# GpSimd's written order ends at the sixth feed-forward pair, and the last spatial-row weights move to activation tiles

## The chip, the cores and the metric

The kernel runs on one core of one Trainium2 chip. The core has five engines with queues of their own: PE (TensorE: matrix products, with its weight loads shown as PEld), DVE (VectorE), ACT (ScalarE), POOL (GpSimd) and SP (SyncE, which only issues transfers). Sixteen DMA engines move data between memory and the on-chip memory. The metric is the time of one execution in microseconds of device time; lower is better.

## The reference

One layer of a diffusion backbone runs over 1024 latent tokens and 256 context tokens of width 1024, all in f32:

```
u    = RMSNorm(x) * (1 + scale1) + shift1
p    = u @ w_in
A    = pooled windows of p (2/4/8/16), minus p, a map per group
B    = su * (W_s RMSNorm(sv) + b)        over chunks of 128 tokens
C    = bidirectional mLSTM, 4 heads of 128, per-head RMSNorm, output gate
x   += gate1 * (sum_r sigmoid(gate_r) * (y_r @ w_branch[r])) @ w_out
x   += gate2 * relu((RMSNorm(x)*(1+scale2)+shift2) @ w_ff1)^2 @ w_ff2
y    = RMSNorm(x)
```

It also returns the final mLSTM states of the context tokens. Branch B's input `sv` (512 columns) is what the code calls the spatial rows. `w_ff1` is 1024 x 4096 and `w_ff2` 4096 x 1024.

## The kernel before

**Arithmetic.** Every large product is made of three matmuls on values split in two: `hi` is the operand cast to the type fp32r by ACT, `lo` is the rest, by a subtraction on DVE; the products are hi·hi, hi·lo and lo·hi. So each weight tile costs one ACT cast and one DVE subtraction before PE can use it.

**Planner.** The kernel is written in a language whose planner simulates the engines' timelines and orders the instructions by what is ready in that simulation, earlier code first. Each engine then executes its own list strictly in order. Two things constrain the planner here: `Pinned` (line 35) wraps an engine so that the instructions issued through it keep their written order on that engine; and buffers come from pools with a fixed number of slots, so that an instruction that writes a new tile waits until a slot of the pool is free.

**Pools that matter.** `sp` has 59 slots of 128x512 f32, the activation tiles (`slot`). `wp` holds raw weights (2 slots), and hi and lo weights of 128x1024 (3 slots each); `load_w` fills them. PSUM has three banks for long products (`ps_mm`) and five for the others (`ps_sd`).

**mLSTM heads and spatial rows.** Four heads run one after the other (`head`), each a chain of short steps over PE, DVE, ACT and GpSimd. While one head runs, the planner fills PE with independent products: the projections of later heads, then the spatial rows, then the projections of the pooling branch (`xp`). The spatial rows are computed in two halves of 256 columns (`q`, line 711); each half has two weight sets (`hf`), for the first and the last four of eight k tiles. For each of ten token tiles 24 matmuls accumulate in a `ps_mm` bank, and ACT copies the result to the row tile `vn` (line 725). In the first half each of the ten groups needs a new `vn` slot. The 40 slots of the modulated input `uT` and three slots `rhl` live through all of this; a head has eight slots of queries, keys and values.

**The first feed-forward matrix.** 16 pairs of 128-column blocks (`fp`, line 1324) go through a Strassen-like scheme with seven products in place of eight (`Pair`, `FeedPair`). After a pair's products, `sums` (line 1274) stores the results and forms their sums on DVE: three stores to `scr_h` and one to `scr_c` from ACT, one to `scr_c` and four to `scr_s` from GpSimd. The sums use tiles of `tmp2`, a pool of six slots, five of which one pair takes. `second_sums(fp)` prepares the weight side of the second matrix: SP loads two rows of `w_ff2` into the z slots 10, 11, 14 and 15 (line 1298), GpSimd makes four subtractions, and GpSimd stores the result to `scr_t`. All pairs share these four z slots, so that the load of one waits for the store of the one before. The dictionary `LATE` (line 1323) says after which pair which `second_sums` are issued: none after pairs 0 and 1, (0) after 2, (1, 2) after 3, (3) after 4, (4, 5) after 5, and from there each after its own pair. The whole loop runs with GpSimd pinned.

**The second feed-forward matrix.** Seven products (`PRODUCTS`, line 1356) run over 16 k steps each; a step needs a right tile (`r_fp`, weights) and a left tile (`l_fp`), each loaded by SP, cast by ACT and split by DVE; every four steps a context tile (`c_j`) joins. In the first product the raw tiles of steps 0 to 9 are loaded into z slots that the first matrix leaves: `FREE` names slots 0, 2, 10, 14, 16, 12, 4, 6, 18, 8 for `r`, the next slot for `l`. So `r_2`, `l_2`, `r_3`, `l_3` use the four slots of `second_sums`. The residual rows are brought back into z by GpSimd's transfers (line 1496).

Of the kernel before, what the change touches and what calls it, by code (L numbers as in the profile page):

```python
# [7 lines left out]
F32 = mybir.dt.float32  # L8
F32R = mybir.dt.float32r
AF = mybir.ActivationFunctionType  # L10
ALU = mybir.AluOpType
# [3 lines left out]
P = 128  # L15
D = 1024
KT = D // P
# [31 lines left out]
def hybrid_step(  # L49
# [6 lines left out]
    nc = tc.nc  # L56
    engines = nc.vector, nc.scalar, nc.gpsimd, nc.tensor
    V, A, G, PE = engines
    SP = nc.sync
# [9 lines left out]
    def slot(name, dt=F32R):  # L69
        return sp.tile([P, 512], dt, tag="s", name=name)  # L70
# [4 lines left out]
    def ps_mm(name):  # L75
        return pp.tile([P, 512], F32, tag="mm", name=name, bufs=3)
# [7 lines left out]
    def fetch_w(src, name):  # L84
        raw = wp.tile([P, 1024], F32, tag="raw", name=f"raw_{name}")
        SP.dma_start(raw, src)
        return raw

    def load_w(src, name, raw=None, eng=V):
        raw = fetch_w(src, name) if raw is None else raw  # L90
        hi = wp.tile([P, 1024], F32R, tag="hi", name=f"hi_{name}", bufs=NHL)
        lo = wp.tile([P, 1024], F32R, tag="lo", name=f"lo_{name}", bufs=NHL)
        A.copy(hi, raw)
        eng.tensor_tensor(lo, raw, hi.bitcast(F32), ALU.subtract)
        return hi, lo
# [10 lines left out]
    def split_part(name, g):  # L106
        if g < 2:
            return slot(f"{name}h{g}"), slot(f"{name}l{g}")
        c = slot(f"{name}c")
        return c[:, 0:256], c[:, 256:512]  # L110
# [16 lines left out]
    def rstd_of(ssq, n, name):  # L127
        r = small([P, 16], f"rs_{name}")
        V.tensor_scalar(r[:, :n], ssq, 1.0 / n_of[name[0]], EPS, ALU.mult, ALU.add)  # L129
        G.tensor_tensor(r[:, :n], r[:, :n], neghalf[:, :n], ALU.pow)  # L130
        return r
# [3 lines left out]
    wt = slot("wt")  # L135
    G.memset(wt.bitcast(F32), 0.0)

# [110 lines left out]
    def busy(n):  # L248

        for _ in range(n):  # L250
            PE.matmul(wps, wt[:, 0:P], wt, start=True, stop=True)
# [23 lines left out]

    V, A, G, PE = (Pinned(tc, e) for e in engines)
    busy(30)
# [87 lines left out]
    def gates_of(g):  # L365


        t0, n = GROUPS[g]
        pg = ps_sd(f"pg{g}")
        for k in range(KT):  # L370
            ahi, alo = uT[k][g]
            w = wgs[k // 4][:, k % 4]
            PE.matmul(pg[:, :n], w, ahi, start=k == 0, stop=False)
            PE.matmul(pg[:, :n], w, alo, start=False, stop=k == KT - 1)
        both, low = slot(f"pgs{g}", F32), slot(f"pgl{g}", F32)
        A.copy(both[:, :n], pg[:, :n])
        SP.dma_start(low[0:100, :n], both[4:104, :n])
        gparts[g] = both, low

    def gates_add(g):  # L380
        t0, n = GROUPS[g]
        both, low = (t[:, :n] for t in gparts[g])
        V.scalar_tensor_tensor(zr[0][:, t0 : t0 + n], both[0:36], bgt[:, 0:1], low[0:36], ALU.add, ALU.add)
        V.tensor_tensor(zr[1][:, t0 : t0 + n], both[64:100], low[64:100], ALU.add)
# [46 lines left out]
    gates_of(2)  # L431
    V, A, G, PE = engines
    gates_add(2)

    def chunks(ap):
        return ap.rearrange("p (c t) -> p c t", t=P)
# [11 lines left out]
    V.scalar_tensor_tensor(zf, zf, 0.0, z4, ALU.min, ALU.subtract)  # L448
    G.memset(z4, 1.0)
    G.memset(chunks(z4)[0:32, :, 0:1], 0.0)  # L450
# [61 lines left out]
    for nm, idx, groups in (("k", I_K, 3), ("v", I_V, 3), ("q", I_Q, 1)):  # L512
        w1, lst = begun[f"{nm}1"] = load_w(w_in[idx + 1], f"{nm}1"), []
        if nm == "q":
            PE = Pinned(tc, nc.tensor)
# [16 lines left out]
    PE = nc.tensor  # L532
# [16 lines left out]
    for g in range(3):  # L549
        t0, n = GROUPS[g]  # L550
        r = slot(f"rhl{g}")
# [154 lines left out]
            qkv = head_proj(h + 1)  # L706


    vn = []
    vsq = cp.tile([P, NT, 2], F32, name="vsq")  # L710
    for q in range(2):
        wq = [load_w(w_sv[q, hf], f"sv{q}_{hf}") for hf in range(2)]
        for i in range(NT):
            g, o = (i * P) // 512, (i * P) % 512
            if q == 0:
                vn.append(slot(f"vn{i}", F32))
            ps = ps_mm(f"sv{q}_{i}")
            for k in range(KT):
                whi, wlo = wq[k // 4]
                s = slice((k % 4) * 256, (k % 4 + 1) * 256)  # L720
                uh, ul = uT[k][g]
                PE.matmul(ps[:, :256], uh[:, o : o + P], whi[:, s], start=k == 0, stop=False)
                PE.matmul(ps[:, :256], ul[:, o : o + P], whi[:, s], start=False, stop=False)
                PE.matmul(ps[:, :256], uh[:, o : o + P], wlo[:, s], start=False, stop=k == KT - 1)
            A.copy(vn[i][:, q * 256 : (q + 1) * 256], ps[:, :256])
            A.activation(ps[:, 256:512], ps[:, :256], AF.Square, accum_out=vsq[:, i, q : q + 1])
    vs1 = small([P, 16], "vs1")[:, :NT]
    V.reduce_sum(vs1, vsq, axis=mybir.AxisListType.X)
    r = rstd_of(vs1, NT, "v")
# [181 lines left out]
    def tmp2(name, dt=F32):  # L911
        return q1.tile([P, 512], dt, tag="s", name=name, bufs=6)
# [158 lines left out]
    for ri, r in enumerate(ORDER):  # L1071
        scr = (scr_ya, scr_yb, scr_yc)[r]
        ys = [[] for _ in range(4)]
        for g in range(3):
            for kc in range(4):
                t0, n = GROUPS[g]
                raw = tmp2(f"yr{r}_{kc}_{g}")
# [5 lines left out]
                hi, lo = split_part(f"y{r}_{kc}", g)  # L1083
# [3 lines left out]
        for d in range(KT):  # L1087
            if d % 2 == 0:
                wb = [load_half(w_branch[r, d // 2][:, i * 512 : i * 512 + 512], f"wb{r}_{d}_{i}") for i in range(2)]
            for g in range(3):  # L1090
# [4 lines left out]
                for kc in range(4):  # L1095
                    yh, yl = ys[kc][g]
                    whi, wlo = wb[kc // 2]
                    o = kc % 2 * 256 + (d % 2) * P
                    s = slice(o, o + P)
# [194 lines left out]
    def second_sums(fp):  # L1294

        q = [zs(i) for i in (10, 11, 14, 15)]
        for r in range(2):
            SP.dma_start(zs(10 + 4 * r, 2), w_ff2[2 * fp + r])
        b11, b12, b21, b22 = q
        for out, x, y in ((b11, b12, b11), (b12, b22, b12), (b22, b22, b11), (b21, b22, b21)):  # L1300
            G.tensor_tensor(out, x, y, ALU.subtract)
        for r in range(2):
            G.dma_start(scr_t[fp][:, 2 * r : 2 * r + 2, :], zs(10 + 4 * r, 2).rearrange("p (q c) -> p q c", c=512))
# [18 lines left out]
    G = Pinned(tc, nc.gpsimd)  # L1322
    LATE = {0: (), 1: (), 2: (0,), 3: (1, 2), 4: (3,), 5: (4, 5)}
    for fp in range(NFP):
# [6 lines left out]
        del pairs[fp]  # L1331
        for late in LATE.get(fp, (fp,)):
            second_sums(late)
    G = nc.gpsimd


    pa.close()
# [262 lines left out]
```

## Time and profile before

| | us |
|---|---|
| median of 3 runs | 1958.27 (1958.17 to 1959.2) |
| the profiled execution | 1958.53 |
| its span in the trace | 1956.7 |
| PE busy | 1906.7 |
| DVE busy | 1309.8 |
| ACT busy | 851.3 |
| POOL busy | 366.6 |

The profile shows one execution. A row of a timeline gives start, length, engine, line, operation, output and input, and in brackets how long the engine was idle before it and what ended that wait. Lines that go through `Pinned` all carry line 43, so operations there are told apart by their tiles. A wait in the trace is put down to what came last.

### The profile page before, as it was taken

To read this page: it belongs to the slowest core of one execution; us is meant where nothing else is said; L and a number is where in the kernel's file an instruction comes from. 1 tells how busy PE (TensorE), PEld (TensorE's weight loads), DVE (VectorE), ACT (ScalarE), POOL (GpSimd) and SP (SyncE) were. 2 spreads that over 40 slices of the span, in tenths; PEclk is the share of its full clock that TensorE was granted. 3 is DMA by queue.
4 is the path that set the end of the run, shared out by engine and by line. 5 is a ranking of instruction groups with operands and counts; after the bars stand their busy time and mean duration, and the time that the engine had idled before them with its cause. 6 is when DMAs were issued, how large, how long until landed. Compare 5 with 4: busy or idle time off the path is not lost.

```text
span 1956.7 us, 28251 instructions
## 1 busy us (share of the span) xinstructions
PE 1906.7 (97%) x10142; PEld 1629.2 (83%) x10142; DVE 1309.8 (67%) x2238; ACT 851.3 (44%) x1771; POOL 366.6 (19%) x393
## 2 busy tenths in 40 slices
PE   8999999999999999999999999999999689999998
PEld 5888888988888888888888878888888578888886
DVE  6575345578797779867675597777777563654665
ACT  6444356533343333442133465445445354443443
POOL 2100000073032324200000001454434400000003
PEclk9999999999999999999999999999999889999999
DMA  9111111125444445289433324677666975655544
GB/s 370 73 60 43 35 38 42 55 87 192 142 157 140 141 140 173 103 304 310 150 113 125 120 91 151 221 269 269 229 222 222 328 255 154 201 176 156 161 137 160
DMA packets 155078, 318.57 MB, mean 163 GB/s; under 512 B 18190, under 2 KB 42482, under 8 KB 154938
## 3 DMA queue, kind: packets, MB, share of 16 engines
q1 hardware_dynamic: 109082, 223.35, 34.9%
q0 software_dynamic: 17824, 57.75, 7.9%
q10 hardware_dynamic: 28032, 35.67, 5.1%
q8 instruction: 79, 1.29, 0.3%
q14 instruction: 61, 0.50, 0.1%
HBM read 220.21 MB, written 95.98 MB: 162 GB/s over the span
## 4 chain that ended last, share of the span: by engine, by line
PE 93%; DMA 3%; ACT 1%; DVE 1%; issue 1%; POOL 0%; SPq 0%; ACTq 0%; POOLq 0%; DVEq 0%
PE w L1467 6%; PE w L1468 6%; PE w L1469 6%; PE fT L934 3%; PE fT L936 3%; PE fT L935 3%; PE pb L1100 3%; PE pb L1101 3%; PE pb L1102 3%; PE fT_g L936 2%; PE fT_g L934 2%; PE fT_g L935 2%; PE fB L934 2%; PE fB L935 2%; PE fB L936 2%; PE po L1228 2%
## 5 line engine op out<-in xcount | busy, mean ns | idle before, releaser
L43 POOL TENSOR_TENSOR z<-z 128x512 f32<-128x512 f32 x64 | 91.2, 1425 | 42.8 <-DMA z<-in_w_ff 39.4
L579 POOL PARTITION_ALL_REDUCE acc<-acc x16 | 54.7, 3458 | 224.3 <-DVE acc L573 139.6
L991 DVE TENSOR_TENSOR z<-z 128x512 f32<-128x512 f32 x120 | 89.0, 742 | 2.7
L573 DVE SCALAR_TENSOR_TENSOR acc<-z,scond,acc 128x512 f32<-128x512 f32 x112 | 82.2, 780 | 0.0
L1421 POOL TENSOR_TENSOR rs_y<-rs_y,neghalf 128x1 f32<-128x1 f32 x10 | 9.4, 940 | 344.3 <-DVE rs_y L1420 344.3
L1017 ACT ACTIVATE z<-z 128x512 f32<-128x512 f32 x56 | 35.4, 632 | 66.5 <-DVE z L1000 19.0
L1267 ACT ACTIVATE z<-z 128x512 f32<-128x512 f32 x64 | 40.4, 631 | 51.6 <-DVE z L1000 26.7
L130 POOL TENSOR_TENSOR rs_h<-rs_h,neghalf 128x4 f32<-128x4 f32 (+1 forms) x12 | 10.9, 910 | 214.2 <-DVE rs_h L129 214.1
L43 POOL DMA_DIRECT2D scr_s<-x x48 | 26.6, 555 | 127.5 <-DVE x L1286 112.3
L1106 DVE TENSOR_TENSOR sg<-pb,sg 128x512 f32<-128x512 f32 (+1 forms) x48 | 28.7, 600 | 24.8 <-PE pb L1102 24.8
L1268 ACT ACTIVATE z<-z 128x512 f32<-128x512 f32 x64 | 40.2, 629 | 1.1
L925 ACT CAST hi_wb<-raw_wb 128x512 fp32r<-128x512 f32 x24 | 14.8, 619 | 58.2 <-PE pb L1101 45.9
L782 POOL TENSOR_TENSOR z<-z 128x256 f32<-128x256 f32 (+13 forms) x20 | 34.7, 1745 | 13.7 <-ACT z L767 5.5
L1230 DVE TENSOR_TENSOR po<-po,gt 128x512 f32<-128x512 f32 (+1 forms) x24 | 14.6, 608 | 33.8 <-PE po L1229 29.6
L624 DVE SCALAR_TENSOR_TENSOR z<-z,dmb,kv 128x129 f32<-128x129 f32 x56 | 17.2, 346 | 28.1 <-PE kv L613 27.9
L580 POOL TENSOR_TENSOR acc<-acc,bt 1x512 f32<-1x512 f32 x16 | 23.0, 1452 | 59.1 <-issue 59.1
L1233 ACT ACTIVATE po<-z 128x512 f32<-128x512 f32 (+1 forms) x24 | 12.7, 529 | 39.9 <-DVE z L1232 32.5
L1107 DVE TENSOR_TENSOR z<-z,sg 128x512 f32<-128x512 f32 (+1 forms) x48 | 28.6, 600 | 1.1
L681 DVE TENSOR_TENSOR den<-den,gcol 128x2 f32<-128x2 f32 x40 | 6.0, 158 | 34.5 <-ACT den L680 34.3
L43 POOL DMA_DIRECT2D scr_c<-xc x16 | 11.7, 734 | 84.4 <-DVE xc L1289 78.3
L606 DVE TENSOR_TENSOR z<-tv,gcol 128x512 f32<-128x512 f32 (+1 forms) x24 | 14.1, 600 | 19.0 <-ACT z L603 18.7
L1000 DVE TENSOR_TENSOR z<-z 128x512 f32<-128x512 f32 x30 | 24.2, 805 | 0.0
(5360 smaller groups left out, 7283.4 us busy)
## 6 DMA issues: line engine op xcount, KB each, us to landing
z<-in_w_ff SPq DMA_DIRECT2D x64, 512.0 KB, 5.3
z<-in_w_ada SPq DMA_DIRECT2D x64, 256.0 KB, 3.0
scr_t<-z POOLq DMA_DIRECT2D x32, 512.0 KB, 3.8
z<-in_w_in SPq DMA_DIRECT2D x28, 512.0 KB, 4.4
scr_g<-z ACTq DMA_DIRECT2D x48, 256.0 KB, 2.0
sg<-scr_g SPq DMA_DIRECT2D x48, 256.0 KB, 4.5
scr_h<-z ACTq DMA_DIRECT2D x48, 256.0 KB, 3.4
scr_s<-x POOLq DMA_DIRECT2D x48, 256.0 KB, 3.5
```

What stands on the lines that cost most here:

```text
L43: return self.tc.keep_in_program_order(getattr(self.eng, op)(*args, **kw))
L573: V.scalar_tensor_tensor(acc[j], raw, scond[:, k, j : j + 1], acc[j], ALU.mult, ALU.add)
L934: PE.matmul(ps, whi[:, s], ahi, start=first and k == ks[0], stop=False)
L935: PE.matmul(ps, whi[:, s], alo, start=False, stop=False)
L936: PE.matmul(ps, wlo[:, s], ahi, start=False, stop=end and k == ks[-1])
L991: V.tensor_tensor(out, x, y, op)
L1100: PE.matmul(pb[:, :n], whi[:, s], yh, start=kc == 0, stop=False)
L1101: PE.matmul(pb[:, :n], whi[:, s], yl, start=False, stop=False)
L1102: PE.matmul(pb[:, :n], wlo[:, s], yh, start=False, stop=kc == 3)
L1467: PE.matmul(banks[j], h_[:, s], rh, start=fp == 0, stop=False)
L1468: PE.matmul(banks[j], l_[:, s], rh, start=False, stop=False)
L1469: PE.matmul(banks[j], h_[:, s], rl, start=False, stop=fp == NFP - 1)
```

## The change

There are two edits. In the first feed-forward loop GpSimd is given back to the planner after pair 5 (the last key of `LATE`) rather than after the loop: its instructions from pair 6 on, the `second_sums` and the stores of `sums`, are no longer held to the written order. In the spatial rows, the last of the four weight sets (second half, last four k tiles) is no longer split into the hi and lo slots of `wp` but into four tiles of `sp`, in two halves of 512 columns; the other three sets are as before. The matmuls and their operands' values are the same.

```diff
+    def sv_weights(q, hf):
+
+        name = f"sv{q}_{hf}"
+        if (q, hf) != (1, 1):
+            hi, lo = load_w(w_sv[q, hf], name)
+            return [(hi[:, i * 256 : i * 256 + 256], lo[:, i * 256 : i * 256 + 256]) for i in range(4)]
+        raw = fetch_w(w_sv[q, hf], name)
+        ws = []
+        for j in range(2):
+            hi, lo, r = slot(f"hi_{name}{j}"), slot(f"lo_{name}{j}"), raw[:, j * 512 : j * 512 + 512]
+            A.copy(hi, r)
+            V.tensor_tensor(lo, r, hi.bitcast(F32), ALU.subtract)
+            ws += [(hi[:, i * 256 : i * 256 + 256], lo[:, i * 256 : i * 256 + 256]) for i in range(2)]
+        return ws
+
...
     for q in range(2):
-        wq = [load_w(w_sv[q, hf], f"sv{q}_{hf}") for hf in range(2)]
+        wq = [sv_weights(q, hf) for hf in range(2)]
...
-                whi, wlo = wq[k // 4]
-                s = slice((k % 4) * 256, (k % 4 + 1) * 256)
+                whi, wlo = wq[k // 4][k % 4]
...
         for late in LATE.get(fp, (fp,)):
             second_sums(late)
-    G = nc.gpsimd
+        if fp == max(LATE):
+            G = nc.gpsimd
```

More of the change, by code (lines that the diff above doesn't have):

```diff
@@ L718, in hybrid_step @@
             for k in range(KT):
-                whi, wlo = wq[k // 4]
-                s = slice((k % 4) * 256, (k % 4 + 1) * 256)
+                whi, wlo = wq[k // 4][k % 4]
                 uh, ul = uT[k][g]
-                PE.matmul(ps[:, :256], uh[:, o : o + P], whi[:, s], start=k == 0, stop=False)
-                PE.matmul(ps[:, :256], ul[:, o : o + P], whi[:, s], start=False, stop=False)
-                PE.matmul(ps[:, :256], uh[:, o : o + P], wlo[:, s], start=False, stop=k == KT - 1)
+                PE.matmul(ps[:, :256], uh[:, o : o + P], whi, start=k == 0, stop=False)
+                PE.matmul(ps[:, :256], ul[:, o : o + P], whi, start=False, stop=False)
+                PE.matmul(ps[:, :256], uh[:, o : o + P], wlo, start=False, stop=k == KT - 1)
             A.copy(vn[i][:, q * 256 : (q + 1) * 256], ps[:, :256])
```

## The prediction

> **What bounds the kernel now.** I read the page's head first, then the waits of PE (TensorE's matmul queue), then a table of stretches, and last the rows around the two places that the change touches.
>
> The head and the chain that ended last:
>
> ```profile
> span 1956.7 us, 28251 instructions
> PE 1906.7 (97%) x10142; PEld 1629.2 (83%) x10142; DVE 1309.8 (67%) x2238; ACT 851.3 (44%) x1771; POOL 366.6 (19%) x393
> PE 93%; DMA 3%; ACT 1%; DVE 1%; issue 1%; POOL 0%; SPq 0%; ACTq 0%; POOLq 0%; DVEq 0%
> ```
>
> PE is the bound: it carries 93% of the chain and idles 1956.7 - 1906.7 = 50.0 us. An edit that touches no matmul can only win part of those idle microseconds, or add to them. GpSimd (POOL, 19% busy) matters through what it holds up. The waits of PE (columns: us in total, times, longest):
>
> ```profile
> PE w L1467 <- ACT r_2h L1366: 18.0, 1, 18.0
> ...
> PE w L1467 <- ACT c_0h L1366: 4.0, 1, 4.0
> ```
>
> Nearly half of PE's idle time is one wait of 18.0 us, for the third right-hand tile (r_2) of the second feed-forward matrix. The stretches (us, then busy time and instruction count of PE, PEld, DVE, ACT, POOL, then PE's granted clock, DMA share, GB/s):
>
> ```profile
> 313.00:338.00 25.00, 20.98 (x172) 19.95 (x171) 8.62 (x30) 15.47 (x58) 2.24 (x3) 1.00 0.21 67
> 338.00:365.00 27.00, 27.00 (x229) 26.72 (x228) 17.79 (x47) 15.36 (x53) 0.36 (x2) 1.00 0.03 11
> 1300.00:1350.00 50.00, 50.00 (x268) 43.28 (x267) 38.75 (x55) 25.13 (x48) 25.96 (x29) 1.00 0.75 265
> 1540.00:1584.00 44.00, 20.88 (x74) 15.73 (x73) 19.56 (x28) 16.31 (x30) 13.99 (x20) 0.69 0.84 302
> 1540.00:1622.00 82.00, 58.88 (x241) 47.23 (x240) 39.03 (x59) 35.23 (x63) 14.91 (x21) 0.83 0.82 286
> 1554.00:1572.00 18.00, 0.58 (x2) 0.00 (x0) 1.39 (x2) 1.33 (x3) 1.87 (x3) 0.50 0.95 333
> 1584.00:1936.00 352.00, 352.00 (x1555) 291.56 (x1554) 198.24 (x326) 147.64 (x263) 12.03 (x17) 1.00 0.57 177
> ```
>
> Between 1540 and 1584, where the first feed-forward matrix hands over to the second, PE does 74 matmuls in 44 us. At the pace of the next stage (352.00 / 1555 = 0.2264 us each) they need 16.8 us, so this handover costs **27.2 us**: the waits and the slow clock behind them (0.50 during the wait). Why r_2 is late (GpSimd's, SP's and ACT's timelines):
>
> ```profile
> 1548.85 5.99 POOL L43 TENSOR_TENSOR z<-z 128x512 f32<-128x512 f32 x4
> 1554.79 1.09 POOL L43 DMA_DIRECT2D scr_t<-z  x2
> 1563.38 0.56 SPq L1375 DMA_DIRECT2D z<-in_w_ff  x1
> 1571.90 0.62 ACT L1366 CAST r_2h<-z 128x512 fp32r<-128x512 f32 x1 [5.78 <-DMA z<-in_w_ff]
> ```
>
> r_2 is loaded into the z slots in which second_sums(15) works. GpSimd computes those sums last of all, writes them out at 1554.79, and only then can SP load r_2 (1563.38); it is cast at 1571.90.
>
> **The change, edit by edit.** *GpSimd's order.* No instruction is added or removed; from pair 6 on, the planner may place GpSimd's four subtractions per pair (second_sums) ahead of the pair's own stores (sums), instead of behind them. What holds them now, in GpSimd's and SP's timelines of pairs 10 and 11, then two starts from the fast stretch:
>
> ```profile
> 1423.60 6.09 POOL L43 TENSOR_TENSOR z<-z 128x512 f32<-128x512 f32 x4
> 1434.49 0.87 SPq L1298 DMA_DIRECT2D z<-in_w_ff  x2
> 1445.36 0.56 POOL L43 DMA_DIRECT2D scr_s<-x  x1 [9.32 <-DVE x L1286]
> ...
> 1448.32 6.08 POOL L43 TENSOR_TENSOR z<-z 128x512 f32<-128x512 f32 x4
> 1300.43 1.29 POOL L43 TENSOR_TENSOR z<-z 128x512 f32<-128x512 f32 x1 [0.61 <-DMA z<-in_w_ff]
> ...
> 1349.84 1.30 POOL L43 TENSOR_TENSOR z<-z 128x512 f32<-128x512 f32 x1 [0.26 <-DMA z<-in_w_ff]
> ```
>
> SP fetches the weights of the sums of pair 11 at 1434.49, but GpSimd stands at its store of pair 11 until 1445.36 and subtracts at 1448.32: the load is there and the written order holds the work back. Pairs 4 to 7 show the pace without that hold: starts at 1300.43 (4) and 1349.84 (7), three steps in 49.4 us, 16.5 us each, limited by the loads. From 1349.84, eight more steps bring second_sums(15) to about 1482 and its stores to about 1494, some 46 us before PE needs r_2. So r_2, l_2, r_3 and l_3 can be loaded ahead and the wait goes.
>
> What is late next? The context tile c_0 (4.0 us of the waits) stands behind DMA that is nearly full (0.95 of the engines during the wait). The 82 us from 1540 to 1622 hold the whole first product (241 matmuls, 54.6 us at 0.2264) and move 82 x 286 = 23.5 MB. About 2.7 MB of it goes earlier (the last sums' load and store, four tiles of 256 KB), which leaves 20.8 MB; at the 333 GB/s of the wait that takes 62.5 us, 7.9 us over PE's 54.6. Much of it belongs to the next product and to the residual rows, and isn't urgent. So 0 to 7.9 us stay; I take 4. **Gain: 27.2 - 4 = 23** (19 to 27).
>
> What the earlier sums collide with is VectorE (DVE). A DVE operation just ahead of the sums of pair 13, two subtractions beside them, and PE's row at the one place where such a subtraction is seen to hold PE:
>
> ```profile
> 1472.84 0.68 DVE L971 TENSOR_TENSOR z<-z,fB 128x512 f32<-128x512 f32 x1
> 1473.44 3.91 DVE L917 TENSOR_TENSOR a_14l<-z,a_14h 128x512 fp32r<-128x512 f32 x2
> 1532.84 0.50 PE L936 MATMUL fT<-T3h,s_15l 128*128 128x512 f32 x1 [0.23 <-DVE s_15l L917]
> ```
>
> A DVE subtraction takes 1.96 us beside the sums, where the operation of the same size ahead of them takes 0.68, but PE feels it only where the tile is wanted at once (0.23 us). In 1300 to 1350 three sums fall at shifting places of the pair and PE is busy 50.00 of 50.00 us. So the collisions cost between 0 and 9 x 0.23 = 2 us; by the nearer row I take 0. The Trainium skill (SBUF — State Buffer, section Who interferes with whom) says that GpSimd and a DVE operation with two SBUF inputs lock each other out for a whole instruction. It speaks against moving the sums; the stretched pair above agrees. If each of the 36 moved subtractions blocked PE for its full 1.3 us, this page's rule would take 47 us; the 1300 to 1350 row speaks against that.
>
> *The last spatial-row weights.* One 128x1024 cast on ACT and one subtraction on DVE become two of 128x512 each (both engines idle in a third or more of 313 to 365, so nothing), and one of three weight buffers is freed for later sets. But they now need four of the 59 activation tiles, and these are short here. By the code, 40 hold the modulated input, 3 the rank-one rows and 16 the tiles of two heads: none is left. The trace shows it (DVE's, ACT's and PE's timelines):
>
> ```profile
> 320.23 0.43 DVE L660 TENSOR_TENSOR z<-z,kq 128x256 f32<-128x256 f32 x1
> 320.69 0.37 ACT L725 COPY vn<-sv 128x256 f32<-128x256 f32 x1
> ...
> 324.67 0.37 ACT L725 COPY vn<-sv 128x256 f32<-128x256 f32 x1 [0.77 <-PE sv L724]
> ...
> 361.89 0.46 ACT L725 COPY vn<-sv 128x256 f32<-128x256 f32 x1
> 312.48 1.05 ACT L93 CAST hi_sv<-raw_sv 128x1024 fp32r<-128x1024 f32 x1 [0.31 <-PE sv L723]
> 327.74 0.28 PE L722 MATMUL sv<-hi_sv,u6h 128*128 128x256 f32 x1
> 327.86 0.28 PE L723 MATMUL sv<-hi_sv,u6l 128*128 128x256 f32 x1
> ...
> 328.57 0.39 PE L675 MATMUL pv<-z,w 128*128 128x129 f32 x2
> ```
>
> A row tile (vn) is copied out at 320.69, 0.03 us after head 2's last reader lets its tile go. The second half's groups (24 matmuls, 0.12 us apart, 2.88 us each) are what PE does while heads 2 and 3 wait for their own chains: nine groups end between 324.67 and 361.89, 25.9 us of filler. The last set's high half is ready at 313.5 now. With four tiles to find it is ready when head 3 gives tiles back, near 350 to 365 by the order of the code; until then only the first halves of three groups (three PSUM banks), 4.3 us, can run. So 21.6 us of filler move behind. That isn't all loss: the filler also holds the heads up. Head 2's product pv, whose inputs end at 320.66, starts at 328.57 behind two groups, so head 2 can end about 7 us sooner, which pays for the 7.2 us of filler lost there. In head 3 (338 to 365) 14.4 us are lost, and the stretch can't fall below DVE's 17.8 us in it, 9.2 less than now; I take 8. **Loss: 14.4 - 8 = 6** (from 21.6, if nothing shortens, down to -4.0, if the idle time of 313 to 338 went too).
>
> **Sum.** The profiled execution took 1958.53 us (span 1956.7 and 1.8 around it), 0.3 above the median of 1958.27. 1958.5 - 23 + 6 = **1941.5 us**.
>
> **The rivals.**
> (1) *The rows starve fully*: the heads don't shorten and all 21.6 us show: 1958.5 - 23 + 21.6 = 1957.1. For it: no free tile. Against: the pv that waited 7.9 us behind filler.
> (2) *DMA takes the place of the sums*: c_0 and the tiles behind it come late, all 7.9 us stay: 1958.5 - 19.3 + 6 = 1945.2. For it: DMA share 0.95 at 333 GB/s. Against: not all 20.8 MB are urgent.
> (3) *Slower: GpSimd's freed order runs ahead of its data.* If the planner thinks the sums cheaper than they are and puts two of them before each pair's stores, GpSimd needs 2 x 16.5 = 33 us for a pair of 24.7 us (1423.60 to 1448.32). The stores come 8.3 us later with every pair; over the five pairs that ten sums last, 41.5 us.
>
> ```profile
> scr_s<-x POOLq DMA_DIRECT2D x48, 256.0 KB, 3.5
> ```
>
> The stores (issued by 1423.60, landed 3.5 us later by the page's row of DMA issues) free tiles that DVE fills again just before 1445.36; some 17 us of delay stay unseen. Past that DVE stands at its sums, and PE behind it: 41.5 - 17 = 24.5 us, 1941.5 + 24.5 = 1966. It decides as soon as the planner takes a step for less than 24.7 / 2 = 12.4 us. Against it: a real step is 16.5 us, and between 1300 and 1350 sums and stores alternate without a loss.
> (4) *It doesn't do what it says*: the planner leaves the sums where they are and only the tiles' cost shows: 1958.5 + 6 = 1964.5. Against it: the same planner already lets SP fetch 13.8 us ahead (1434.49 against 1448.32).
> (5) *The page's lock on PE's path*: 1941.5 + 47 = 1988; the trace gives it little.
>
> **How the numbers follow.** Forecast 0.55 (its own range 1931 to 1951), rival 1 0.12, rival 2 0.13, rival 3 0.11, rival 4 0.08, rival 5 0.01. 0.2% (3.9 us), about what a measurement of this kernel can tell from no change, puts the bounds at 1954.4 and 1962.2. Faster: 0.55 + 0.13 = 0.68. Same: rival 1, 0.12. Slower: 0.11 + 0.08 + 0.01 = 0.20. The range must hold the forecast and rivals 1 and 2 (0.80): its low end is the full 27.2 us with 4.0 more from the rows, 1927; its high end rival 1 and a little, 1959.
>
> **What would show it.** Right: second_sums(15) ends on GpSimd before 1510, PE's wait for r_2 is under 1 us, and the stretch from the last matmul of the first matrix to the end of the first product is 55 to 63 us; the second half's last weights are cast after 335 in two halves, and the end of head 3 comes 0 to 22 us later against its own matmul count. Wrong: a wait of DVE for GpSimd's stores during pairs 7 to 14 (rival 3), sums still behind each pair's stores (rival 4), casts of the last weights before 300 without row tiles waiting, or PE waits between 1225 and 1540 where there were none.

## The result, and the profile after

The changed kernel takes **1947.31 us** (median of 4 runs, 1945.39 to 1950.28) against 1958.74 (1958.17 to 1959.22) for the kernel before in the same comparison: a ratio of 0.9943, 95% interval 0.9926 to 0.996. That is 11.4 us faster; the forecast was 17, and the time lies inside the range. The profiled execution took 1945.39 us, 13.1 less than that of before, and this section divides those 13.1. One run of e8 below (2175.84 us, at a granted clock of 0.82) was disturbed and is left out of its figures.

The head of the page, of the kernel after:

```profile
span 1943.6 us, 28266 instructions
PE 1907.7 (98%) x10142; PEld 1630.1 (84%) x10142; DVE 1302.8 (67%) x2239; ACT 848.2 (44%) x1772; POOL 367.7 (19%) x393
```

PE does the same 10142 matmuls and idles 35.9 us (1943.6 - 1907.7) in place of 50.0. Its waits, after:

```profile
PE th L690 <- ACT z L689: 8.4, 3, 3.3
PE fc L948 <- ACT hc L1285: 3.5, 2, 1.8
...
PE sv L736 <- ACT sv L740: 2.2, 1, 2.2
```

The waits for r_2 (18.0 us) and c_0 (4.0) are gone from the list. `th` and `sv`, in the mLSTM heads and the rows beside them, have grown, and `fc`, a product of the first feed-forward matrix, is new: there the prediction had expected nothing.

To see how much each place gives or takes, I cut the profiled executions at three points: the first matmul of `mx` (the first product behind the heads and the rows), the first of `fB` (the first feed-forward matrix begins) and the first of `w` (the second begins). "First matrix" is from `fB` to `w`, "tail" from `w` to the end of the span. All times are us.

| kernel | profiled execution | `mx` begins at | first matrix | tail |
|---|---|---|---|---|
| before | 1958.53 | 415.2 | 397.2 | 416.0 |
| after | 1945.39 | 419.9 | 405.7 | 389.7 |
| difference | -13.1 | +4.7 | +8.5 | -26.3 |

The three add up to the difference, since from `mx` to `fB` both take 728.3. **The handover gave 26.3, the rows cost 4.7, and the first matrix lost 8.5.** The windows that hold these stretches, after (us; busy time and instructions of PE, PEld, DVE, ACT, POOL; PE's clock, DMA share, GB/s):

```profile
313.00:338.00 25.00, 16.96 (x129) 16.10 (x129) 12.28 (x42) 16.36 (x59) 1.70 (x2) 0.93 0.22 71
338.00:365.00 27.00, 26.85 (x226) 26.48 (x225) 16.94 (x55) 17.16 (x66) 1.37 (x3) 1.00 0.09 26
1148.20:1553.90 405.70, 397.80 (x2064) 340.76 (x2065) 318.18 (x466) 207.53 (x386) 154.39 (x179) 0.99 0.62 221
1557.00:1612.00 55.00, 54.45 (x240) 44.62 (x240) 30.52 (x49) 26.03 (x48) 5.96 (x11) 1.00 0.89 309
```

The last row begins 3 us behind the start of the second matrix: 240 matmuls in 55.00 us, about as many as the first product has, almost without a gap. The row above it is the first matrix. The same view of before, cut at its own two points:

```profile
1143.50:1540.70 397.20, 394.02 (x2065) 337.93 (x2066) 311.17 (x463) 207.85 (x384) 148.33 (x172) 1.00 0.61 216
```

The same work (2064 and 2065 matmuls recorded) has PE idle for 7.9 us rather than 3.2, and busy for 397.80 rather than 394.02 at a granted clock of 0.99 rather than 1.00. So 4.7 of the 8.5 us are waits, and the other 3.8 are matmuls that last longer at the lower clock. Cut into windows of 25 us, the matrix has two with a clock under 0.95 (the last two rows), after:

```profile
1148.20:1173.20 25.00, 22.05 (x113) 18.11 (x114) 24.76 (x47) 18.17 (x36) 0.48 (x1) 0.99 0.13 43
1173.20:1198.20 25.00, 24.97 (x109) 20.26 (x109) 20.82 (x36) 13.41 (x24) 2.24 (x5) 0.94 0.43 140
...
1473.20:1498.20 25.00, 22.30 (x111) 19.00 (x111) 18.90 (x24) 11.03 (x22) 15.12 (x16) 0.93 0.61 227
```

The second lies at new waits. The first doesn't: it follows waits at the start of the matrix that before has as well, where they end without a lower clock:

```profile
1143.50:1168.50 25.00, 22.05 (x115) 18.12 (x116) 24.75 (x46) 18.20 (x36) 0.51 (x1) 1.00 0.14 47
```

So about 25 x 0.06 = 1.5 us of the 8.5 belong to this one execution, and some 7 are left to explain.

**Where they come from.** SP's queue while pairs 10 to 12 run, after (a row gives the start, and how long the group of transfers took to be issued, the waits between them included):

```profile
1385.41 15.52 SPq L1312 DMA_DIRECT2D z<-in_w_ff  x3
1401.02 1.12 SPq L963 DMA_DIRECT2D z<-in_w_ff  x2
1403.56 19.89 SPq L1312 DMA_DIRECT2D z<-in_w_ff  x3
```

L1312 is a load for `second_sums` (L1298 before), L963 the load of a pair's own weights (L949 before). A load for the sums can start only when the sums ahead of it have left their z tiles, and SP stands at it until then: 15.52 and 19.89 us. The pair's own weights, issued behind it at 1401.02, must wait all the same, although the last subtraction that reads their tiles, of pair 9, had ended at 1390.71 by DVE's timeline of after:

```profile
1390.02 0.69 DVE L931 TENSOR_TENSOR s_9l<-z,s_9h 128x512 fp32r<-128x512 f32 x1
```

ACT's timeline and then PE's, after:

```profile
1410.02 0.62 ACT L930 CAST a_11h<-z 128x512 fp32r<-128x512 f32 x1 [7.37 <-DMA z<-in_w_ff]
...
1412.55 0.38 ACT L1285 ACTIVATE hc<-fc 128x256 f32<-128x256 f32 x1
```

```profile
1412.99 0.39 PE L948 MATMUL fc<-u20c,a_10h 128*128 128x256 f32 x1 [1.71 <-ACT hc L1285]
```

The weights of pair 11, issued at 1401.02, are cast at 1410.02, after ACT stood 7.37 us for them; `hc` is behind that cast in ACT's order, and PE waits for `hc`. The wait of PE names ACT, the wait of ACT names a DMA, and the DMA was late because of what stood ahead of it on SP. So the theory to test is: the sums moved forward, and their loads took the place of other loads in an in-order queue. The rival is that the earlier sums hold DVE up, as the lock rule that the prediction quoted would have it.

### The profile page after: what moved, and what is told of

It reads as the page before. It is cut to its first block, busy times and chain, and to the rows that moved or that the text cites. A ratio compares the mean times of both kernels' runs of the same rounds, so it can differ in the third digit from the quotient of the medians.

```text
span 1943.6 us, 28266 instructions
## 1 busy us (share of the span) xinstructions
PE 1907.7 (98%) x10142; PEld 1630.1 (84%) x10142; DVE 1302.8 (67%) x2239; ACT 848.2 (44%) x1772; POOL 367.7 (19%) x393
## 4 chain that ended last, share of the span: by engine, by line
PE 91%; DMA 2%; issue 2%; DVE 2%; ACT 2%; POOL 0%; SPq 0%; ACTq 0%; POOLq 0%; DVEq 0%
PE w L1482 6%; PE w L1484 6%; PE w L1483 6%; PE fT L948 3%; PE pb L1115 3%; PE pb L1114 3%; PE pb L1116 3%; PE fT L950 3%; PE fT L949 3%; PE fT_g L948 3%; PE fT_g L949 3%; PE fT_g L950 3%; PE fB L948 2%; PE fB_g L950 2%; PE fB L950 2%
## 5 line engine op out<-in xcount | busy, mean ns | idle before, releaser
L1005 DVE TENSOR_TENSOR z<-z 128x512 f32<-128x512 f32 x120 | 95.9, 799 | 2.7
L796 POOL TENSOR_TENSOR z<-z 128x1024 f32<-128x1024 f32 (+13 forms) x20 | 36.4, 1830 | 18.5 <-ACT z L780 16.2
L796 DVE TENSOR_TENSOR z<-z 128x1024 f32<-128x1024 f32 (+6 forms) x10 | 19.0, 1896 | 9.7 <-ACT z L801 9.5
L606 DVE TENSOR_TENSOR z<-tv,gcol 128x512 f32<-128x512 f32 (+1 forms) x24 | 14.1, 600 | 16.5 <-ACT z L603 16.2
```

Of the source, the lines that this page charges most:

```text
L1005: V.tensor_tensor(out, x, y, op)
```

## The experiments

Every run is compared with the kernel before on its own chip. The points of the table above, for all of them, in one place:

| kernel | profiled execution | `mx` begins at | first matrix | tail |
|---|---|---|---|---|
| before | 1958.53 | 415.2 | 397.2 | 416.0 |
| after | 1945.39 | 419.9 | 405.7 | 389.7 |
| e1 GpSimd's order alone | 1938.63 | 413.0 | 405.4 | 389.3 |
| e2 rows' weights alone | 1965.76 | 421.0 | 397.2 | 417.0 |
| e3 written order, one pair ahead | 1952.48 | 414.6 | 405.9 | 399.0 |
| e4 e1, loads by GpSimd | 1933.21 | 414.3 | 396.8 | 390.7 |
| e5 four tiles held | 1956.22 | 413.5 | 396.7 | 415.0 |
| e6 eight tiles for the rows | 1976.23 | 431.7 | 397.8 | 416.9 |
| e7 e3, loads by GpSimd | 1945.53 | 413.1 | 396.6 | 404.4 |
| e8 after, loads by GpSimd | 1938.99 | 421.2 | 397.1 | 391.0 |
| e9 three pairs ahead, loads by GpSimd | 1931.61 | 414.1 | 397.4 | 390.2 |
| e10 late split alone | 1961.91 | 418.8 | 397.2 | 416.8 |

### e1 and e2: each edit alone

e1 is the kernel before with the change in the loop only:

```diff
             second_sums(late)
-    G = nc.gpsimd
+        if fp == max(LATE):
+            G = nc.gpsimd
```

> Only the GpSimd edit; the spatial rows' weights as before. Theory: the edit wins about 26 us at the handover (23 forecast) and loses about 8.5 us inside the first feed-forward matrix, because SP stands at the loads of second_sums and fetches the pairs' own weights late; the rows' edit costs 4 to 5 us elsewhere. So this kernel takes about 1947 - 4.5 = 1942 to 1943 us, the stretch from the first fB matmul to the last one is about 405 us (397 before) and ACT waits for weights (a_11 to a_15 for z<-in_w_ff). Rival (the two edits depend on each other, the loss in the first matrix comes from the shifted plan behind the rows): about 1934 us, stretch 397 us.

e1: 1940.53 us (1938.63 to 1942.67, 4 runs), ratio 0.9902 (0.9887 to 0.9917). e2 is the kernel after with these lines put back:

```diff
             second_sums(late)
-        if fp == max(LATE):
-            G = nc.gpsimd
+    G = nc.gpsimd
```

> Only the rows' edit. Theory (four activation tiles fewer for the row tiles, so that PE lacks filler between 313 and 365 us): 4 to 6 us slower than before, 1963 to 1964 us, with the whole loss ahead of 420 us (first mx matmul at 420 instead of 415). Rival (the rows' edit is neutral and the 4.7 us come from the planner's order under the other edit): 1958 to 1959 us.

e2: 1964.77 us (10 runs), ratio 1.002 (1.001 to 1.0029). The two edits don't meet: the loss of the first matrix (405.4) and the short tail (389.3) go with GpSimd's order, the late `mx` (421.0) with the rows. e1 has no lower clock at the start of the matrix. Its only window with one lies where pair 11 waits for its weights, and its first matrix is 8.2 us longer than before (405.4 - 397.2):

```profile
1392.10:1417.10 25.00, 21.85 (x105) 18.86 (x104) 16.58 (x23) 9.29 (x18) 13.06 (x16) 0.86 0.70 252
```

By the ratios a gain of 0.98% less a loss of 0.20% makes 0.78%; 0.57% (0.40 to 0.74) was measured for both together, and with the intervals of e1 and e2 (0.83 to 1.13, 0.10 to 0.29) the two agree.

### e4: only the queue of the sums' loads

If SP's queue is the cause, the sums may stay where the planner put them, and only their loads must leave SP. GpSimd can issue them itself: it is the engine that frees the tiles, so what stands behind that wait is its own work alone.

```diff
         for r in range(2):
-            SP.dma_start(zs(10 + 4 * r, 2), w_ff2[2 * fp + r])
+            (G if fp > 5 else SP).dma_start(zs(10 + 4 * r, 2), w_ff2[2 * fp + r])
...
         for late in LATE.get(fp, (fp,)):
             second_sums(late)
-    G = nc.gpsimd
+        if fp == max(LATE):
+            G = nc.gpsimd
```

> e1 with the two loads of each second_sums from pair 6 on issued on GpSimd's queue and not on SP's; the orders of PE, DVE and ACT are those of e1. Theory (SP's queue is what makes the pairs' weights late): ACT's waits for the pairs' weights go, first-matrix stretch back to 397 to 399 us, 1942 - 8 = 1934 us, unless GpSimd, which now stands at the loads itself, holds the stores back. Rival (the collisions of GpSimd's subtractions with DVE, or the DMA engines' load, make the loss): the stretch stays near 405 us.

Measured: **1932.87 us** (1931.33 to 1934.07, 4 runs), ratio 0.9862 (0.9847 to 0.9877), the lowest median of this study. SP's queue, and then the window of the first matrix and that of the tail, of e4:

```profile
1384.04 100.76 SPq L949 DMA_DIRECT2D z<-in_w_ff  x10
```

```profile
1143.90:1540.70 396.80, 393.84 (x2066) 338.04 (x2066) 319.67 (x466) 208.06 (x387) 166.74 (x199) 1.00 0.64 226
1540.70:1931.40 390.70, 381.69 (x1681) 314.94 (x1679) 224.70 (x371) 167.25 (x304) 22.32 (x34) 0.99 0.60 190
```

SP now issues ten weight loads in a row, each when its own tiles are free. The first matrix takes 396.8 us, as before the change (397.2), with the sums nearly as early as in e1 (their last store at 1501.05; in e1 at 1490.28). From 1225 to 1545 the list of PE's waits is empty, and of ACT's waits for weights only one of 1.7 us for pair 5 is left, which the kernel before has as well. So the 8.2 us of e1 were the order on SP, and the rival falls: DVE has the sums beside it here as well, is busy for 319.67 us in the stretch rather than 311.17, and costs PE nothing.

The Trainium skill (DMA: Bandwidth & Descriptors, section Issuing engines are not separate DMA queues) says that starting transfers from several engines "will only save the time on the sequencer it takes to initiate the DMA". By that, as an estimate, e4 should have gained over e1 the issue times of twenty loads, 20 x 0.33 = 6.6 us of an engine that PE doesn't wait for, and not 8.6 us of the first matrix (405.4 - 396.8). The runs show what the sentence leaves out: the wait of a transfer is held by the engine that issues it, with all that stands behind. By another sentence of the same page of the Trainium skill (section Anatomy of one DMA — SWDGE (gpsimd) path) a semaphore wait is done by the issuing sequencer, ahead of the DMA engines; the 15.52 us of SP agree with it.

### e8: the same with both edits

The kernel after with the first hunk of e4.

> Both edits of the change, with the loads of second_sums from pair 6 on issued by GpSimd; orders of PE, DVE and ACT as in the changed kernel. Theory (the three terms add: handover -26, rows +4 to 5, SP's queue 0): e4 + 4.5 = 1937 to 1938 us. Rival (the terms depend on each other): 1933 or less, or 1941 or more.

Measured: 1937.72 us (median of 3 runs), ratio 0.9886 (0.9864 to 0.9908). First matrix 397.1, tail 391.0, `mx` at 421.2: the queue costs the same with the rows' edit in place, and with the rows' edit the kernel takes 4.9 us more than e4 (1937.72 - 1932.87).

### e3, e7 and e9: is it the freed order, or only the earlier sums?

e3 keeps the written order in the whole loop and writes the sums one pair earlier.

```diff
-    LATE = {0: (), 1: (), 2: (0,), 3: (1, 2), 4: (3,), 5: (4, 5)}
+    LATE = {0: (), 1: (), 2: (0,), 3: (1, 2), 4: (3,), 5: (4, 5), 6: (6, 7), 15: ()}
+    LATE.update({n: (n + 1,) for n in range(7, 15)})
```

> The kernel before, GpSimd in written order through the whole loop, but second_sums(n+1) written behind pair n from pair 6 on (two behind pair 6, none behind pair 15). Theory: the handover only needs the last sums to end before about 1540, not 70 us sooner; one pair ahead, second_sums(15) ends near 1530, r_2 comes in time or up to 5 us late, and SP isn't held up because the loads stay one for each pair: 1958 - 22 to 26 = 1932 to 1937 us, first-matrix stretch 397 to 399 us. Rival (DVE and GpSimd collide wherever the sums move, and that makes the 8.5 us): the stretch grows by several us here too and the time is 1940 or more.

This missed. e3 took 1944.76 us (1941.53 to 1952.48, 4 runs), ratio 0.9929 (0.9902 to 0.9956), where 1932 to 1937 was expected. SP's queue, e3:

```profile
1384.59 2.23 SPq L1298 DMA_DIRECT2D z<-in_w_ff  x2
1387.14 1.42 SPq L949 DMA_DIRECT2D z<-in_w_ff  x1
1402.15 0.33 SPq L1298 DMA_DIRECT2D z<-in_w_ff  x1
1402.57 1.59 SPq L949 DMA_DIRECT2D z<-in_w_ff  x1
```

With one pair ahead a load for the sums falls between the two weight loads of a pair. The first goes at 1387.14, the second only at 1402.57. I had thought that a written order would keep the sums' loads behind both; the planner orders SP freely, whatever GpSimd's order is. The first matrix took 405.9. The tail is 399.0, but the profiled run is the slowest of the four, 7.7 us over their median. GpSimd's timeline of e3 has the store of the last sums 8.5 us ahead of the second matrix, which begins at 1551.7; PE's longest wait in the tail stands below it:

```profile
1543.18 1.10 POOL L43 DMA_DIRECT2D scr_t<-z  x2
```

```profile
PE w L1468 <- ACT c_0h L1367: 5.0, 1, 5.0
```

PE doesn't wait for r_2 or l_2 here. It waits for c_0, whose load goes out on SP at 1552.50, right behind loads into the tiles of the sums; in the kernel after it goes out at 1548.00, ahead of the second matrix.

e7 takes the loads off SP, as e4 does:

> e3 (written order, one pair ahead) with the loads of second_sums from pair 6 on issued by GpSimd. Theory (in e3 SP stood 15 us at such a load between the two weight loads of pair 11, and that alone made the stretch 8.7 us longer): stretch back to 397 to 398 us. The handover keeps e3's own price, as second_sums(15) still works there (399 us from the last fB to the end, against 389 to 391 in e1 and e4): about 1941 us. Rival (GpSimd and DVE collide): stretch 405 us.

e7: 1947.01 us (1945.53 to 1952.24, 4 runs), ratio 0.9939 (0.9919 to 0.9959). The first matrix is back at 396.6, as expected, but the tail is 404.4 and not 399. The store of GpSimd's last sums, two windows of the handover and PE's waits, e7:

```profile
1536.36 1.11 POOL L43 DMA_DIRECT2D scr_t<-z  x2
```

```profile
1540.00:1550.00 10.00, 4.94 (x22) 3.75 (x20) 2.22 (x4) 2.49 (x4) 3.07 (x6) 0.99 1.00 308
1550.00:1570.00 20.00, 17.54 (x69) 14.38 (x70) 13.61 (x22) 11.66 (x21) 3.80 (x7) 0.83 1.04 410
```

```profile
PE w L1468 <- ACT l_2h L1367: 7.5, 1, 7.5
...
PE w L1468 <- ACT accU L1432: 3.3, 1, 3.3
```

The sums of pair 15 are stored 3 us before the second matrix begins (1539.3). The loads of r_2 and l_2 then go out into a stretch in which the DMA engines are full (a share of 1.00), and PE waits 7.5 us for `l_2`. The 3.3 us for `accU`, the copy of the first product's result, come later, at 1610, and are not explained. So the expectation of e7, which took e3's tail over, was wrong about the margin, and e9 tries a larger one: written order, loads by GpSimd, and the sums of pair 15 behind pair 12.

```diff
-    LATE = {0: (), 1: (), 2: (0,), 3: (1, 2), 4: (3,), 5: (4, 5)}
+    LATE = {0: (), 1: (), 2: (0,), 3: (1, 2), 4: (3,), 5: (4, 5), 6: (6, 7), 8: (9, 10), 10: (12, 13), 11: (14,), 12: (15,), 13: (), 14: (), 15: ()}
+    LATE.update({7: (8,), 9: (11,)})
```

> GpSimd keeps its written order throughout, but the sums are written earlier, so that those of pair 15 stand behind the twelfth pair's work, and GpSimd starts their loads itself. Theory (what counts is how long before the end of the first feed-forward matrix the last sums and their stores are done, not whether the order is written or free): the stretch of the first matrix 396-398 us, the tail from the first matmul of the second matrix 389-391, the run about 1933. Rival (the freed order does something that a written order doesn't): the tail stays at 399 or more, the run at 1941 or more. Every sum whose loads come sooner than its tiles are free would show as a longer wait of GpSimd, and PE waits between 1145 and 1540 would speak against the theory's first number.

e9: 1936.44 us (1931.61 to 1940.28, 4 runs), ratio 0.989 (0.9871 to 0.9909). The store of GpSimd's last sums of e9, and its two windows:

```profile
1506.07 1.10 POOL L43 DMA_DIRECT2D scr_t<-z  x2
```

```profile
1142.20:1539.60 397.40, 394.21 (x2065) 338.00 (x2065) 309.23 (x465) 207.32 (x386) 167.27 (x199) 1.00 0.64 224
1539.60:1929.80 390.20, 381.56 (x1681) 315.02 (x1679) 224.79 (x371) 166.87 (x304) 22.36 (x34) 0.99 0.61 192
```

First matrix 397.4, tail 390.2, both as the theory expected, in a written order throughout; the median of 1936.44 lies 3 us over the expected 1933, with the profiled run the fastest of the four. It isn't the freedom of the order that pays: sums stored early in a written order give the same short tail. From the rows above, the prediction's row of before and the table: stored 14 us *after* the second matrix begins, a tail of 416.0 (before); 3 us ahead of it 404.4 (e7); 8.5 us ahead 399.0 (e3); 33 us ahead 390.2 (e9: 1539.6 - 1506.1). In the kernel after it is 58 us ahead and 389.7, by GpSimd's timeline of after:

```profile
1493.63 1.30 POOL L1315 TENSOR_TENSOR z<-z 128x512 f32<-128x512 f32 x1
...
1495.96 0.54 POOL L1317 DMA_DIRECT2D scr_t<-z  x1
```

So 3 us are too little and 33 are enough. What a lead of 8.5 us costs is open: the two fastest runs of e3 (1941.53 and 1942.00) lie among those of e1, whose first matrix is as long, so that its tail of 399.0 may belong to the profiled run alone. Whether e4 is truly faster than e9 isn't shown either: their intervals overlap, and their profiled runs stand at 1933.21 and 1931.61.

### e5, e6 and e10: what the rows' edit pays for

The prediction said that the last weights wait for four activation tiles, none of which is free. e5 takes four tiles from the pool at the same place, but leaves the weights where they were: four two-column copies claim the tiles, and a later operation holds them to the last group of the rows.

```diff
+            raw11 = fetch_w(w_sv[1, 1], "sv1_1")
+            hold = [slot(f"hold{i}", F32) for i in range(4)]
+            for t in hold:
+                A.copy(t[:, 0:2], raw11[:, 0:2])
+            wq.append(load_w(None, "sv1_1", raw11))
...
+    for t in hold:
+        V.tensor_scalar(t[:, 0:2], t[:, 0:2], vsq[:, NT - 1, 1:2], None, ALU.mult)
```

> The kernel before, whose weights stay in their old buffers, with four activation tiles taken for nothing: each gets a two-column copy from the raw weights of the last set, and is held until the last row group's square is done. Theory (the price of the rows' edit is four activation tiles fewer, not where the weights lie): the first mx matmul comes 4 to 6 us later than before, near 420, and head 3's first transposes (tk) come near 331 in place of 337. Rival (the price is the late cast of the last set itself): that cast runs at 312 as before and mx starts at 413 to 415.

e5: 1958.4 us (8 runs), ratio 0.9993 (0.9983 to 1.0004): no price, `mx` at 413.5. The theory as I had put it for this run, a shortage of tiles as such, fell. ACT's timeline of e5 shows why:

```profile
310.73 1.05 ACT L93 CAST hi_sv<-raw_sv 128x1024 fp32r<-128x1024 f32 x1 [0.30 <-PE sv L731]
...
340.35 0.27 ACT L719 COPY hold<-raw_sv 128x2 f32<-128x2 f32 x1
```

The first held tile comes only at 340.35, so tiles are short indeed; but the weights were split at 310.73, and nothing that PE needs soon stands behind the held tiles. e6, again from the kernel before, goes the other way and puts both sets of the second half into activation tiles (`if q != 1` in place of `if (q, hf) != (1, 1)`, with the loop as before):

> The rows' edit doubled: both weight sets of the second half in activation tiles (eight in place of four), GpSimd's order as before. Theory (tiles are what the second half waits for): with 40 + 3 + 8 + 10 tiles taken there are not eight left before head 3 gives back most of its own, so the second half's casts end after 365 and mx starts well behind 420, 425 to 435. Rival (a change of the plan without a dose): mx near 420 or 415.

e6: 1975.04 us (2 runs), ratio 1.0077 (1.0053 to 1.0101), `mx` at 431.7. ACT's timeline of e6 has the first of its four half splits, which every group of the second half needs:

```profile
336.59 0.65 ACT L719 CAST hi_sv<-raw_sv 128x512 fp32r<-128x512 f32 x1
```

Four tiles cost 5.8 in e2 (421.0 - 415.2) and eight 16.5 (431.7 - 415.2): here no group of the second half can begin ahead of 336.59. Last, e10 leaves the last set in its own tiles and makes only its split late, through one activation tile:

```diff
+            hold = [slot("hold0", F32)]
+            A.copy(hold[0][:, 0:2], raw11[:, 0:2])
+            A.copy(raw11[:, 0:2], hold[0][:, 0:2])
+            wq.append(load_w(None, "sv1_1", raw11))
```

> The tiling of before, with the last set of the spatial rows' weights in its own tiles as there, but its split into halves made to wait for one activation tile (a two-column copy through such a tile and back), so that only the time of the split changes. Theory (the price of the rows' edit is the late split of the last set, whatever tile it lies in): split near 340 us, the next phase (mx) begins at 417-421, as in the run with the rows' edit alone (421.0). Rival (the price is something else in the edit, such as the tiles it takes from the heads): mx at 413-415, as before (415.2).

e10: 1962.04 us (8 runs), ratio 1.0015 (1.0004 to 1.0026), where e2 has 1.002 (1.001 to 1.0029). The split on ACT, and the window of head 2, of e10:

```profile
335.53 1.05 ACT L93 CAST hi_sv<-raw_sv 128x1024 fp32r<-128x1024 f32 x1
```

```profile
313.00:338.00 25.00, 17.50 (x134) 16.64 (x134) 11.35 (x38) 17.38 (x61) 1.70 (x2) 0.93 0.09 30
```

A split that comes 24.8 us later than in e5 (335.53 against 310.73) moves PE's busy time in that window to 17.50, from 20.98 before, and `mx` to 418.8, 3.6 us later than before. That is most of what the rows' edit costs (4.7 in after, 5.8 in e2); by the medians, each against the kernel before on its chip, it is 2.6 of e2's 4.0 us. Whether the rest is the tiles that the weights then hold, or the spread of single profiled runs (`mx` begins between 413.0 and 415.2 in the six kernels whose rows are as before), stays open.

## Why the prediction was right, and where it was wrong

**The handover: right, and mis-sized low.** It forecast 23 us from 27.2 less 4 for DMA that stays full; 26.3 came. Second_sums(15) ended at 1494.9 (it said about 1482) and was stored at 1496 (about 1494), r_2 isn't waited for, and the first product needs 55 us, the lower end of its 55 to 63. The term that was too large is the 4 us of DMA. The window of 20 us in the middle, after:

```profile
1550.00:1570.00 20.00, 19.90 (x89) 16.13 (x88) 12.37 (x20) 10.01 (x18) 9.37 (x17) 1.00 1.00 348
```

DMA is as full as it was (1.00, 348 GB/s), yet PE works for 19.90 of 20.00 us: what is loaded then is not what PE wants next. Rival 2, with its 7.9, took the volume for a need. e7 shows the same load with a need in it, and there it costs.

**The rows: right in mechanism, wrong in the place, and right in the sum by luck.** It forecast 6, out of 21.6 us of delayed filler less what the heads shorten; 4.7 came in after, 5.8 in e2. The last set was split in two halves after 335, as it said, at these times on ACT, after:

```profile
335.60 0.64 ACT L719 CAST hi_sv<-raw_sv 128x512 fp32r<-128x512 f32 x1
...
342.92 0.62 ACT L719 CAST hi_sv<-raw_sv 128x512 fp32r<-128x512 f32 x1 [1.36 <-PE rb L646]
```

Head 3 begins sooner, by about the forecast 7 us: its first `tk` stands at 330.00 after (the second row below) and at 336.85 before (the first).

```profile
336.85 0.38 PE L598 MATMUL tk<-cst,kT 128*128 128x128 f32 x2
```

```profile
330.00 1.06 PE L598 MATMUL tk<-cst,kT 128*128 128x128 f32 x4
```

But the forecast let head 2 come out even and head 3 lose 6. In the windows it is the reverse: from 313 to 338 PE is busy for 16.96 us rather than 20.98, a loss of 4.0, and from 338 to 365 for 26.85 rather than 27.00. The weights were there by 343, and not near 350 to 365, so that in head 3 filler was at hand again, and its shortening was not needed to pay for anything. Two terms that were both too large (14.4 and 8) left a difference that was nearly right.

**The collisions: the step that failed.** The prediction put "the collisions cost between 0 and 9 x 0.23 = 2 us", looked for them on DVE, and took 0. On DVE it was right: beside the sums a pair of subtractions takes 3.07 us in the kernel after, as DVE's timeline has it, and e4 shows that PE doesn't feel such pairs:

```profile
1490.58 3.07 DVE L931 TENSOR_TENSOR a_14l<-z,a_14h 128x512 fp32r<-128x512 f32 x2
```

By the lock rule in its full form (rival 5) this would have been 47 us; the rule's stretch of DVE agrees with the rows, a price on PE doesn't. What it left out is that the sums' loads and the pairs' own weights share one queue: when the sums move forward, their loads move ahead of those weights, with waits of 15.52 and 19.89 us in the rows above. It named SP's fetch at 1434.49 as proof that "the load is there", and did not ask what would stand behind that load when it had to wait. That was some 7 of the 8.5 us in the profiled run, and 8.2 in e1, and its sign "PE waits between 1225 and 1540 where there were none" is the one that came true.

**The rivals.** (1) is out: 4.7 and not 21.6. (2) is out, as told. (3) had the right shape on the wrong engine: the freed order did run ahead of what the pairs need, but through SP's loads and at 7 to 8 us; DVE's waits for GpSimd's stores between 1225 and 1545 come to 0.4 us, as before. (4) is out by e1. The sum, against its own profiled run: -23 + 6 + 0 = -17 was forecast, -26.3 + 4.7 + 8.5 = -13.1 came.

## What to carry to other kernels

A transfer that moves forward takes its wait along, and the queue that issues it is in order: before moving work, list what stands behind its loads, and give a load that must wait for a buffer to the engine that frees the buffer (8.6 us here, e1 against e4). A step that must be done before a handover needs only enough lead for the loads that use its buffers (3 us was too little, 33 enough). A scarce buffer costs only what waits behind it: four tiles held for nothing cost 0 here, and the same wait in front of weights that PE needs cost 4 to 6 us.

## What the runs showed of the hardware

- A queue of transfers stands in its own order even where later transfers could go: SP stood 15.52 and 19.89 us at loads whose tiles were not free, and a weight load behind them, whose tiles were free from 1390.71, went out at 1401.02.
- Loads issued by GpSimd land a little later than SP's of the same size, and the first matrix shows no cost of it (396.8 in e4). The table of transfers of e4 (count, size, median us from issue to landing):

```profile
z<-in_w_ff SPq DMA_DIRECT2D x44, 512.0 KB, 5.5
...
z<-in_w_ff POOLq DMA_DIRECT2D x20, 512.0 KB, 6.1
```

- Full DMA by itself doesn't hold PE up: with the DMA engines at 1.00 and 348 GB/s PE was busy for 19.90 of 20.00 us (after), and at 402 GB/s for 26.00 of 26.00 us (e9, from 1540 to 1566).
- Short gaps of PE cost twice, and not every time. Behind two gaps of 0.90 and 1.79 us, 2.3 us apart, the matmuls of the kernel after take 0.41 us each in place of 0.28, from 1493.3 to 1496.7, and then are as fast as before. PE's timeline of after:

```profile
1491.81 0.39 PE L948 MATMUL fc<-u20c,a_13h 128*128 128x256 f32 x1 [1.79 <-ACT hc L1285]
1492.03 0.28 PE L949 MATMUL fc<-u20c,a_13h 128*128 128x256 f32 x1
...
1494.16 0.41 PE L949 MATMUL fc<-u25c,a_13h 128*128 128x256 f32 x1
```

  The waits at the start of the matrix were followed by a lower clock in after (0.94), e3 (0.96) and e6 (0.96), and by none in the nine other kernels. The Trainium skill (TensorE: Matmul & The Clock Gate, section HAM oscillation — how this bites in real kernels) states the rule as "no PE-idle gaps >~3.4µs"; here gaps about half as long, close together, stand ahead of the slow matmuls.
- Where the gaps are more, the clock falls further: in e6, whose heads ran short of filler, it was 0.73 from 313 to 338:

```profile
313.00:338.00 25.00, 15.31 (x91) 14.02 (x91) 10.26 (x38) 16.29 (x59) 1.70 (x2) 0.73 0.08 30
```
